# Tree attention on one core: where the last four heads' and one early quad's K and Q are transposed

## The chip, the cores and the metric

The kernel runs on one core of one Trainium2 chip. The metric is the device time of one execution in microseconds (us); of several executions the median is given. Engines are named as the profile names them: PE (TensorE, matmuls and transposes), PEld (its weight loads), DVE (VectorE), ACT (ScalarE), POOL (GpSimd, which here issues nearly all transfers), SP (SyncE).

## The reference, cut to what matters

Attention with 8 batches of 12 heads, 512 positions, 64 dimensions, in float32. A position attends to itself and to its ancestors in a binary heap.

```python
mask = np.zeros((seq, seq))
for i in range(seq):
    mask[i, i] = 1
    parent = i
    while parent > 0:
        parent = (parent - 1) // 2
        mask[i, parent] = 1
scores = np.einsum('bhqd,bhkd->bhqk', Q, K) * scale      # scale = 1/sqrt(64)
scores = scores + (1 - mask) * (-1e9)
weights = np.exp(scores - np.max(scores, axis=-1, keepdims=True))
weights = weights / (np.sum(weights, axis=-1, keepdims=True) + 1e-10)
return np.einsum('bhqk,bhkd->bhqd', weights, V)
```

## The kernel before

The 96 heads are worked on in **pairs** (two heads, index `i`, 0 to 47), **quads** (four heads, index `q`, 0 to 23, two pairs each) and **octets** (eight heads, index `o`, 0 to 11). Q, K and V are loaded from float32 into bf16 tiles of one octet each; K and Q come in halves of an octet, that is, by the quad. A position has at most nine keys that count, so a pair needs two score tiles only: one against the 128 keys nearest the root (`scores1`), one against a packed selection of the others (`scores2`). In each, a first matmul adds a mask code and a second adds the product of K and Q; ACT then takes the exponential of 128x1024 scores at once (lines 396 and 422).

For the scores, K and Q must lie with the dimension across the partitions. Both are brought there by transposes on PE, which write one PSUM tile, `kqp`, of two halves:

- `first_pair(i)` (the first 8 pairs, octets 0 and 1): 8 transposes of K and 8 of Q of one pair; DVE copies both halves to SBUF (line 322).
- `keys_of(q)` (from quad 4 on): 16 transposes of K for both pairs of a quad, line 308, one pair in each half of `kqp`; DVE copies the tile to `kT` (line 322).
- `queries_of(q)`: 16 transposes of Q for both pairs, line 357, into the second half of `kqp`; DVE copies that to `qT` (line 366).

There is one `kqp` tile, so each of these has to wait until DVE has copied out what the one before it wrote. In the last steps the space of `kqp` is also used for the output of pairs 45 and 47 (line 432).

`values(i)` multiplies the exponentials of pair i with V, which has to be spread out first to the packed order of the keys: POOL copies the top part (line 246), DVE the leaves (line 260) and a part of level 7 (lines 275 and 283), ACT the rest of level 7 (line 275). A column of ones beside V gives the sums, and `norm(i)` divides by them on DVE (lines 467 and 470). The output tile of `values` in PSUM is single too. `store` sends a quad's result out: POOL for most quads, SP and ACT for the last one.

The order of instructions on each engine is that in which the Python code issues them: the schedule is set by hand, and semaphores are put in where data demands them. One step `i` of the main loop issues the scores of pair i, a share of spreading on ACT, the values and the normalization of pair i-1, the transposes for pairs further ahead, a share of spreading on DVE, and then the next part of POOL's list of transfers. With the two conditions in lines 595 to 600, `keys_of(q)` comes in step 2q-3 and `queries_of(q)` in step 2q-2, both after the values and the normalization; quad q's first scores come in step 2q. So quad 4's K is issued in step 5 and quad 23's K and Q in steps 43 and 44.

Of the kernel before, what the change touches and what calls it, by code (L numbers as in the profile page):

```python
# [124 lines left out]
def kernel(  # L125
# [12 lines left out]
    NQ = B * H // 4  # L138
    NP = 2 * NQ
# [61 lines left out]
    OLD = 2  # L201
# [56 lines left out]
    def spread_leaves(o, upper, h0=0, h1=8):  # L258

        nc.vector.tensor_copy(  # L260
            out=tile_pair(o, 64 if upper else 0, h0, h1, upper),
            in_=vsts[o][64:128, h0:h1, upper:3 + upper:2, :],
        )
# [7 lines left out]
    def spread_l7(copy, o, quad, h0=0, h1=8):  # L271

        slot = 2 * (quad % 2)
        lower = quad < 2
        copy(  # L275
            out=tile_pair(o, 0, h0, h1, 1)[32 * quad:32 * quad + 32] if lower
            else tile_pair(o, 64, h0, h1, 0)[32 * quad - 64:32 * quad - 32],
            in_=swapped(vsts[o][32:64, h0:h1, slot + (not lower), :], D if lower else -D),
        )

    def spread_l7_over(o):

        nc.vector.tensor_copy(
            out=tile_pair(o, 64, 0, 8, 0),
            in_=swapped(vts[o % NV][0:64, 0:8, VCOL[3]:VCOL[3] + D], -D),
        )
# [23 lines left out]
    def transpose_keys(dst, i):  # L310
        for t in range(4):
            for a in range(2):
                transpose_one(dst, i, a, t, _slot_layout(t)[1], ksts, perms[t])

    def evac_units(name):
        kq = work.tile([P, 2, 16, 32], bf16, name=name)
        src = kqp[:, :, :]
        src = bass.AP(
            src.tensor, src.offset + 32 * _psum_unit(0),
            [list(src.ap[0]), [1024, 2], [32 * (_psum_unit(8) - _psum_unit(0)), 2], [1, 256]],  # L320
        )
        nc.vector.tensor_copy(  # L322
            out=kq[:, :, :, :].rearrange("p k (x y) c -> p k x (y c)", x=2), in_=src
        )
        return kq

    def first_pair(i):

        transpose_keys(kqp[:, 0, :], i)
        for t in range(4):  # L330
            for a in range(2):
                transpose_one(
                    kqp[:, 1, :], i, a, t, [_psum_unit(4 * QPOS[t] + j) for j in range(4)],
                    qsts, turns[:, :],
                )
        kq = evac_units("kq")
        kTs[i] = kq[:, 0, :, :]
        qTs[i] = kq[:, 1, :, :].rearrange("p (t u) c -> p t (u c)", t=4)

    def keys_of(q):  # L340

        for r in range(2):
            transpose_keys(kqp[:, r, :], 2 * q + r)
        kT = evac_units("kT")
        for r in range(2):
            kTs[2 * q + r] = kT[:, r, :, :]

    def queries_of(q):

        st = qsts[q // 2][:, 4 * (q % 2):4 * (q % 2) + 4, :, :].rearrange(  # L350
            "p (y x) t d -> p y (x t) d", y=2
        )
        for t in range(4):
            for j in range(2):
                for a in range(2):
                    dst = kqp[64 * a:64 * a + 64, 1, :]
                    nc.tensor.transpose(  # L357
                        out=bass.AP(
                            dst.tensor, dst.offset + 128 * QPOS[t] + 16 * j,
                            [list(dst.ap[0]), [512, 2], [32, 4], [1, 16]],  # L360
                        ),
                        in_=st[:, a, 4 * j + t, :],
                        identity=qperm,
                    )
        qT = work.tile([P, 2, 4, 128], bf16, name="qT")
        nc.vector.tensor_copy(  # L366
            out=qT[:, :, :, :].rearrange("p r t c -> p (r t c)"), in_=kqp[:, 1, :]
        )
        for r in range(2):
            qTs[2 * q + r] = qT[:, r, :, :]  # L370
# [10 lines left out]
    def scores1(i):  # L381

        sp = psS.tile([P, 2, 512], fp32, name="s1")
        for a in range(2):
            nc.tensor.matmul(  # L385
                out=sp[:, a, :], lhsT=k1code[64 * a:64 * a + 64, :],
                rhs=q1code[64 * a:64 * a + 64, :], start=True, stop=False,
            )
        for a in range(2):
            nc.tensor.matmul(  # L390
                out=sp[:, a, :], lhsT=keys(i, a, TOP),
                rhs=qTs[i][64 * a:64 * a + 64, :, :].rearrange("p t c -> p (t c)"),
                start=False, stop=True,
            )
        et = etpool.tile([P, 2, 4, 128], bf16, name="e1")
        nc.scalar.activation(  # L396
            out=et[:, :, :, :].rearrange("p a t c -> p (a t c)"),
            in_=natural(sp[:, :, :]),
            func=AF.Exp, scale=scale,
        )  # L400
        ets[i] = et

    def scores2(i):

        sp = psS.tile([P, 2, 4, 128], fp32, name="s2")
        for a in range(2):
            nc.tensor.matmul(  # L407
                out=sp[:, a, :, :].rearrange("p t c -> p (t c)"),
                lhsT=k2code[64 * a:64 * a + 64, :], rhs=q2code[64 * a:64 * a + 64, :],
                start=True, stop=False,  # L410
            )
        for tile2, lo, hi in ((2, 32, 192), (0, 192, 320), (1, 320, 384), (3, 416, 512)):
            for a in range(2):
                nc.tensor.matmul(  # L414
                    out=sp[:, a, :, :].rearrange("p t c -> p (t c)")[:, lo:hi],
                    lhsT=keys(i, a, TILE2[tile2]),
                    rhs=qTs[i][64 * a:64 * a + 64, :, :].rearrange("p t c -> p (t c)")[:, lo:hi],
                    start=False, stop=tile2 == 3, skip_group_check=tile2 in (2, 0),
                )
        e2 = etpool.tile([P, 2, 4, 128], bf16, name="e2")[:, :, :, :]  # L420
        e2s[i] = e2
        nc.scalar.activation(  # L422
            out=e2.rearrange("p a t c -> p (a t c)"),
            in_=natural(sp[:, :, :, :]),
            func=AF.Exp, scale=scale,
        )
# [50 lines left out]
    def store(eng, q, h0=0, n=4, step=1):  # L477
        eng.dma_start(  # L478
            out=Or[:, 4 * q + h0:4 * q + h0 + n:step, :],
            in_=ofs[q][:, h0:h0 + n:step, :, :].rearrange("p h t d -> p h (t d)"),  # L480
        )
# [39 lines left out]
    def spread_first(copy, quad, parts):  # L521

        for part in parts:
            if part < 4:
                spread_l7(copy, 0, part, 4 * quad, 4 * quad + 4)
            else:
                spread_leaves(0, part - 4, 4 * quad, 4 * quad + 4)
# [20 lines left out]
    def spread_scalar(i):  # L548

        if i == 1:  # L550
            spread_first(nc.scalar.copy, 1, (0, 1))
        o, quad = divmod(i + 1, 4)
        if 2 <= o < NO and quad == 0:
            spread_l7(nc.scalar.copy, o, 0)
        if i == 4:
            for quad in (0, 1):
                spread_l7(nc.scalar.copy, 1, quad)

    def pool_until(done, wanted):
        while done < wanted:  # L560
            next(program, None)
            done += 1
        return done
# [14 lines left out]
    for i in range(NP + 1):  # L578
        if i < NP:
            scores1(i)  # L580
            scores2(i)
            spread_scalar(i)
        if i == 1:
            first_pair(2)
            spread_first(nc.vector.tensor_copy, 1, (2, 3))
        if i >= 1:
            values(i - 1)
            norm(i - 1)
        if i >= 8 and i % 4 == 0 and i < NP:
            spread_l7_over(i // 4)  # L590

        for n in (1 if i == 0 else i + 2,):
            if n < 4 * OLD:
                first_pair(n)
        q, r = divmod(i + 3, 2)
        if 2 * OLD <= q < NQ and r == 0:
            keys_of(q)
        q, r = divmod(i + 2, 2)
        if 2 * OLD <= q < NQ and r == 0:
            queries_of(q)  # L600
        if i == 0:
            spread_first(nc.vector.tensor_copy, 0, range(6))
        spread_vector(i)
        if steps < NO:
            steps = pool_until(steps, min((i + 11) // 4, NO))
        else:
            steps = pool_until(steps, min(steps + 2, NO + (i - 2) // 2 - (NQ - 1 - BEHIND)))
        if i == NP - 1:
            store(nc.sync, NQ - 1, 0, 3, 2)
# [32 lines left out]
```

## Time and profile before

| what | value |
|---|---|
| median of 5 runs (lowest, highest) | 136.88 us (135.82, 138.01) |
| the profiled execution's own time | 136.5 us |
| its span in the trace | 134.7 us |
| PE busy, of the span | 115.6 us (86%) |
| DVE busy | 103.8 us (77%) |
| ACT busy | 105.7 us (78%) |
| POOL busy | 95.2 us (71%) |
| one exponential (line 396), mean | 1018 ns |
| one evacuation of K (line 322, kT), mean | 684 ns |
| one evacuation of Q (line 366), mean | 686 ns |
| bytes moved by the DMA engines | 32.20 MB |

How to read it: a busy share is over the whole span, and PE's end times are modelled, so it isn't PE at its peak. "L308 MATMUL kqp<-ptile,kst x16" is a group of 16 instructions of line 308 that write `kqp` and read `ptile` and `kst`; what stands in brackets is the time its engine sat idle before it and what ended that. The slices of the page are 40 equal parts of the span, each 3.37 us; a digit 9 means busy for 90% or more. The chain of work that ended last is followed back from the last instruction.

### The profile page before, as it was taken

The page shows a single profiled execution, that of the slowest core. Times are in us where ns is not written, and L with a number is a line of the kernel's source. Part 1 is how long each engine was busy: PE and PEld are TensorE (multiplying, and loading weights), DVE is VectorE, ACT ScalarE, POOL GpSimd, SP SyncE. Part 2 cuts the span into 40 slices and gives each one's busy share as a digit, 9 for nine tenths or more (in the row PEclk, how much of TensorE's full clock was granted, in tenths as well). Part 3 has the DMA queues.
Part 4 walks back from the last instruction along what each step waited for, and adds up shares of the span by engine and source line. Part 5 has one row for each costly group of instructions (what it writes and reads, how often), then busy time and mean ns, then how long its engine had stood idle before and what let it go on. Part 6 is the DMA issues. An engine that isn't in the chain of part 4 may idle for free.

```text
span 134.7 us, 5515 instructions
## 1 busy us (share of the span) xinstructions
PE 115.6 (86%) x2409; PEld 79.8 (59%) x2409; DVE 103.8 (77%) x218; ACT 105.7 (78%) x113; POOL 95.2 (71%) x140
## 2 busy tenths in 40 slices
PE   4986996599999998998998999999996988969920
PEld 1434674467576776766675675767664765746610
DVE  5548989568969879798789789798797689659450
ACT  4155989479799799899799797997985997879920
POOL 6939989598697974984886697596696498295100
PEclk9999999999999999999999999999999999999998
DMA  3999999999999999999999999999999999999982
GB/s 105 230 165 192 191 196 201 199 204 195 202 198 227 334 203 212 338 210 204 338 218 201 318 242 199 298 263 200 286 274 202 263 297 201 249 382 364 373 297 90
DMA packets 36858, 32.20 MB, mean 239 GB/s; under 512 B 1458, under 2 KB 33890, under 8 KB 36834
## 3 DMA queue, kind: packets, MB, share of 16 engines
q0 software_dynamic: 35520, 30.68, 120.5%
q1 hardware_dynamic: 754, 0.72, 1.7%
q10 hardware_dynamic: 560, 0.46, 1.1%
q8 instruction: 19, 0.31, 0.8%
q14 instruction: 5, 0.04, 0.1%
HBM read 37.88 MB, written 12.58 MB: 375 GB/s over the span
## 4 chain that ended last, share of the span: by engine, by line
DMA 43%; PE 24%; DVE 11%; ACT 7%; POOL 6%; issue 5%; ACTq 0%; POOLq 0%
DMA vst<-in_V_dram 26%; DMA kst<-in_K_dram 9%; DMA qst<-in_Q_dram 8%; PE ob L441 8%; PE kqp L308 4%; ACT e L396 4%; DVE of L470 4%; ACT e L422 4%; PE s L385 3%; PE s L407 3%; PE s L390 2%; PE s L414 2%; POOL kst L220 2%; DVE vt L275 2%; PE kqp L357 2%
## 5 line engine op out<-in xcount | busy, mean ns | idle before, releaser
L396 ACT ACTIVATE e<-s 128x1024 bf16<-128x1024 f32 x48 | 48.8, 1018 | 17.8 <-PE s L390 17.6
L422 ACT ACTIVATE e<-s 128x1024 bf16<-128x1024 f32 x48 | 48.6, 1013 | 0.0
L441 PE MATMUL ob<-vt,e 128*128 128x65 bf16 (+1 forms) x920 | 37.1, 197 | 1.2 <-DVE vt L275 0.9
L246 POOL COPY vt<-vst 32x512 bf16<-32x512 bf16 (+1 forms) x52 | 30.9, 595 | 10.0 <-DMA vst<-in_V_dram 8.1
L441 PEld LDWEIGHTS <-e 128*128 128x128 bf16 (+1 forms) x960 | 30.5, 102 | 7.9 <-issue 1.0
L470 DVE TENSOR_TENSOR of<-ob,rec 128x512 f32<-128x512 f32 x46 | 31.8, 692 | 1.6
L220 POOL DMA_DIRECT2D kst<-in_K_dram x24 | 18.8, 784 | 11.4 <-DMA vst<-in_V_dram 9.1
L478 POOL DMA_DIRECT2D out_dram<-of x23 | 17.5, 767 | 4.8 <-DVE of L470 4.2
L308 PE MATMUL kqp<-ptile,kst 128*64 128x128 bf16 x384 | 16.2, 222 | 5.3 <-DMA kst<-in_K_dram 2.3
L407 PE MATMUL s<-codes 64*128 64x512 bf16 x96 | 18.5, 378 | 2.1 <-ACT e L422 1.9
L467 DVE RECIPROCAL rec<-ob 128x8 f32<-128x8 f32 x46 | 9.6, 208 | 13.9 <-PE ob L441 13.1
L385 PE MATMUL s<-codes 64*128 64x512 bf16 x96 | 18.9, 390 | 0.5
L308 PEld LDWEIGHTS <-kst 128*64 128x64 bf16 x384 | 12.7, 111 | 7.7 <-DMA kst<-in_K_dram 4.5
L414 PEld LDWEIGHTS <-kT 64*128 64x128 bf16 x320 | 13.3, 94 | 6.0
L322 DVE COPY kT<-kqp 128x1024 bf16<-128x1024 bf16 x20 | 13.7, 684 | 2.9 <-PE kqp L308 2.8
L236 POOL DMA_DIRECT2D qst<-in_Q_dram x20 | 14.1, 707 | 2.4 <-issue 1.1
L407 PEld LDWEIGHTS <-codes 64*128 64x128 bf16 x96 | 7.4, 94 | 14.0 <-issue 8.4
L390 PE MATMUL s<-qT,kT 64*128 64x512 bf16 x80 | 15.3, 376 | 0.0
L414 PE MATMUL s<-qT,kT 64*128 64x160 bf16 (+3 forms) x320 | 14.7, 209 | 0.0
L275 ACT COPY vt<-vst 32x1024 bf16<-32x1024 bf16 (+1 forms) x14 | 13.6, 970 | 1.3 <-DMA vst<-in_V_dram 1.3
L220 POOL DMA_DIRECT2D vst<-in_V_dram x13 | 11.7, 904 | 4.1 <-DMA qst<-in_Q_dram 1.3
L366 DVE COPY qT<-kqp 128x1024 bf16<-128x1024 bf16 x20 | 13.7, 686 | 0.3
(34 smaller groups left out, 96.7 us busy)
## 6 DMA issues: line engine op xcount, KB each, us to landing
out_dram<-of POOLq DMA_DIRECT2D x23, 512.0 KB, 10.6
kst<-in_K_dram POOLq DMA_DIRECT2D x23, 256.0 KB, 11.3
qst<-in_Q_dram POOLq DMA_DIRECT2D x23, 256.0 KB, 9.7
vst<-in_V_dram POOLq DMA_DIRECT2D x11, 512.0 KB, 12.5
vst<-in_V_dram POOLq DMA_DIRECT2D x2, 256.0 KB, 7.5
first_k<-in_K_dram SPq DMA_DIRECT2D x1, 256.0 KB, 3.2
first_q<-in_Q_dram ACTq DMA_DIRECT2D x1, 256.0 KB, 4.1
out_dram<-of SPq DMA_DIRECT2D x1, 256.0 KB, 3.7
```

Of the source, the lines that this page charges most:

```text
L220: nc.gpsimd.dma_start(out=kept[o][:, h0:h0 + n:step, :, :].rearrange("p h t d -> p h (t d)"), in_=src[:, 8 * o + h0:8 * o + h0 + n:step, :],)
L246: eng.tensor_copy(out=vts[o % NV][32 * j:32 * j + 32, h0:h1, VTOP:VTOP + D], in_=vsts[o][0:32, h0:h1, UNITS[TOP + j][1], :],)
L308: nc.tensor.transpose(out=dst, in_=st[i // 4][:, head(i, a), t, :], identity=perm)
L385: nc.tensor.matmul(out=sp[:, a, :], lhsT=k1code[64 * a:64 * a + 64, :], rhs=q1code[64 * a:64 * a + 64, :], start=True, stop=False,)
L390: nc.tensor.matmul(out=sp[:, a, :], lhsT=keys(i, a, TOP), rhs=qTs[i][64 * a:64 * a + 64, :, :].rearrange("p t c -> p (t c)"), start=False, ...
L396: nc.scalar.activation(out=et[:, :, :, :].rearrange("p a t c -> p (a t c)"), in_=natural(sp[:, :, :]), func=AF.Exp, scale=scale,)
L407: nc.tensor.matmul(out=sp[:, a, :, :].rearrange("p t c -> p (t c)"), lhsT=k2code[64 * a:64 * a + 64, :], rhs=q2code[64 * a:64 * a + 64, :] ...
L414: nc.tensor.matmul(out=sp[:, a, :, :].rearrange("p t c -> p (t c)")[:, lo:hi], lhsT=keys(i, a, TILE2[tile2]), rhs=qTs[i][64 * a:64 * a + 6 ...
L422: nc.scalar.activation(out=e2.rearrange("p a t c -> p (a t c)"), in_=natural(sp[:, :, :, :]), func=AF.Exp, scale=scale,)
L441: nc.tensor.matmul(out=ob[lo:hi, a, start_o:start_o + 65], lhsT=e[:, a, QPOS[t], lo:hi], rhs=vt[:, head(i, a), col:col + 65], **flags,)
L470: nc.vector.tensor_tensor(out=ofs[q][:, r:r + 3:2, :, :], in0=vals, in1=rec[:, :, :, :].to_broadcast([P, 2, 4, D]), op=ALU.mult,)
L478: eng.dma_start(out=Or[:, 4 * q + h0:4 * q + h0 + n:step, :], in_=ofs[q][:, h0:h0 + n:step, :, :].rearrange("p h t d -> p h (t d)"),)
```

## The change

Two steps of transposing that the two general conditions placed are now placed by themselves.

- Quad 4 (pairs 8 and 9, `4 * OLD - 2` is 6): `keys_of(4)` leaves step 5 and is issued in step 6, between the scores of pair 6 and the values of pair 5. `queries_of(4)` stays in step 6 behind the normalization of pair 5.
- Quad 23 (pairs 46 and 47): `keys_of(23)` leaves step 43 and is issued in step 44 (`NP - 4`), behind the values and the normalization of pair 43. `queries_of(23)` leaves step 44 and is issued in step 45 (`NP - 3`), between the scores of pair 45 and the values of pair 44.

Where a transposing step goes, its evacuation on DVE goes with it. No instruction is added or removed, and nothing of ACT's, POOL's and SP's order is touched.

```diff
@@ -583,21 +583,28 @@
         if i == 1:
             first_pair(2)
             spread_first(nc.vector.tensor_copy, 1, (2, 3))
+        if i == 4 * OLD - 2:
+            keys_of(2 * OLD)
+        elif i == NP - 3:
+            queries_of(NQ - 1)
         if i >= 1:
             values(i - 1)
             norm(i - 1)
         if i >= 8 and i % 4 == 0 and i < NP:
             spread_l7_over(i // 4)
 
+
         for n in (1 if i == 0 else i + 2,):
             if n < 4 * OLD:
                 first_pair(n)
         q, r = divmod(i + 3, 2)
-        if 2 * OLD <= q < NQ and r == 0:
+        if 2 * OLD < q < NQ - 1 and r == 0:
             keys_of(q)
         q, r = divmod(i + 2, 2)
-        if 2 * OLD <= q < NQ and r == 0:
+        if 2 * OLD <= q < NQ - 1 and r == 0:
             queries_of(q)
+        if i == NP - 4:
+            keys_of(NQ - 1)
         if i == 0:
             spread_first(nc.vector.tensor_copy, 0, range(6))
         spread_vector(i)
```

## The prediction

> **What bounds the kernel now.** I read the slices of the page first: is a transfer limit in force all the time?
>
> ```profile
> DMA  3999999999999999999999999999999999999982
> GB/s 105 230 165 192 191 196 201 199 204 195 202 198 227 334 203 212 338 210 204 338 218 201 318 242 199 298 263 200 286 274 202 263 297 201 249 382 364 373 297 90
> HBM read 37.88 MB, written 12.58 MB: 375 GB/s over the span
> ```
>
> The DMA engines are busy from the second slice to the last but one. Pure loads show about 200 GB/s because they arrive as bf16, half the bytes read. So the moment at which the last load lands is set by the bytes ahead of it, not by the engines. The chain in order of time agrees, and tells where this ends:
>
> ```profile
> 93.96 13.08 DMA vst<-in_V_dram
> ...
> 107.33 12.07 DMA kst<-in_K_dram
> 119.40 0.04 issue
> 119.44 0.64 PE kqp L308 x16
> ```
>
> The last K load (heads 4 to 7 of octet 11, that is, pairs 46 and 47) lands at 119.40 us; then computation is on the chain to the end. Next the timeline of PE around it (start, us, instruction, idle before it):
>
> ```profile
> 117.35 0.79 PE L441 MATMUL ob<-vt,e 128*128 128x65 bf16 x20
> 119.44 0.64 PE L308 MATMUL kqp<-ptile,kst 128*64 128x128 bf16 x16 [1.30 <-DMA kst<-in_K_dram]
> 120.01 0.39 PE L385 MATMUL s<-codes 64*128 64x512 bf16 x2
> ```
>
> PE stands 1.30 us before the K transposes for pairs 46 and 47, and pair 44's scores, which need nothing of that load, stand behind them. ACT shows what that is worth:
>
> ```profile
> 117.88 1.02 ACT L422 ACTIVATE e<-s 128x1024 bf16<-128x1024 f32 x1
> 118.78 1.03 ACT L275 COPY vt<-vst 32x1024 bf16<-32x1024 bf16 x1
> 120.72 1.02 ACT L396 ACTIVATE e<-s 128x1024 bf16<-128x1024 f32 x1 [0.91 <-PE s L390]
> 124.76 1.02 ACT L396 ACTIVATE e<-s 128x1024 bf16<-128x1024 f32 x1
> ```
>
> Only 0.91 of the 1.30 us is idle time of ACT; the copy of line 275 fills the rest. The line at 124.76 is pair 46, the first that needs the late load. Last, DVE in the same stretch, since both evacuations of the late heads go through it:
>
> ```profile
> 120.12 0.69 DVE L322 COPY kT<-kqp 128x1024 bf16<-128x1024 bf16 x1 [1.01 <-PE kqp L308]
> 120.84 0.42 DVE L260 COPY vt<-vst 64x1024 bf16<-64x1024 bf16 x1
> 121.28 0.72 DVE L275 COPY vt<-vst 32x1024 bf16<-32x1024 bf16 x1
> 122.03 0.21 DVE L467 RECIPROCAL rec<-ob 128x8 f32<-128x8 f32 x1
> 122.27 0.69 DVE L470 TENSOR_TENSOR of<-ob,rec 128x512 f32<-128x512 f32 x1
> 122.99 0.42 DVE L283 COPY vt<-vt 64x1024 bf16<-64x1024 bf16 x1
> 123.44 0.69 DVE L366 COPY qT<-kqp 128x1024 bf16<-128x1024 bf16 x1
> ```
>
> After the K load DVE has no gap until the Q evacuation ends at 124.13. It will be the next limit.
>
> **What the Trainium skill says.** (1) "TensorE: Matmul & The Clock Gate", Step-by-step: what each phase is for: matmuls stay in program order, only weight loads are pulled ahead. The trace agrees: nothing overtakes the transposes waiting at 119.44. (2) "SBUF — State Buffer", SBUF: two separate sides: VectorE in a two-port mode and GpSimd take one port pair in turn, the later one standing still. Line 283's ten copies take 421 to 766 ns, line 260's 26 (two widths) 291 to 743, which fits but doesn't prove it; this is my range for those copies. (3) "DMA: Bandwidth & Descriptors", Anatomy of one DMA: some 2 us of a transfer are fixed, mostly waiting until the last byte is confirmed. The last store, 128 KB, took 3.0 us from issue: the end follows the last normalization by about that.
>
> **The change, part by part.** The profiled execution took 136.5 us, 1.8 more than its span of 134.7; the median is 136.88, so the profile ran 0.4 faster than the median.
>
> *K step of quad 4 (pairs 8 and 9), from the end of step 5 to between scores and values of step 6.* Before, its 16 transposes waited 1.18 us (start 26.28) for the evacuation of pair 7, and pair 6's scores stood behind; exp of pair 6 began at 27.56. Now the scores go first: pair 7's transposes start at 24.49 and need 0.57, then 0.61 for scores and 0.10 to ACT: exp at about 25.8. The new wait, the same one until 26.28, has pair 5's values behind it: 26.85 to 27.57. DVE does the K evacuation 26.96 to 27.65 ahead of the normalization; the Q transposes, which reuse the same PSUM tile, wait for that: 27.69 to 28.24, then pair 7's scores, exp at 28.24+0.61+0.10 = 28.95 instead of 29.68. So 0.73 us of lead from pair 7 on. I value it at nothing at the end: PE later stands for K at 108.42 (0.66 us), 113.56 (0.38) and 119.44, times that saturated transfers set. No DMA is issued by the moved step, and POOL's order of issues stays. If that cover were gone, up to 0.73 us would reach the end; a loss I exclude, as pairs 6 and 7 both come earlier.
>
> *K step of quad 23, from step 43 to behind step 44's values.* Removed: the 1.30 us wait. PE: values of pair 42 end issue at 118.07; scores1 of pair 44 follow; scores2 wait for the exp that ends at 118.90, start 118.94, and values of pair 43 start 0.52 later (as 122.71 to 123.23): 119.46 to 120.18. The transposes then start at 120.18, 0.8 after the load has landed: no wait. ACT: exp(44) starts when the copy ends, 119.83, not 120.72: 0.89 earlier. Then at its pace of 0.92 per exp: 120.75, exp1(45) 121.67, exp2(45) 122.59 to 123.61.
>
> DVE's order changes too. The normalization of pair 42 ends at 119.11; the two spread copies (0.42+0.72) no longer wait for the K evacuation: 119.14 to 120.30. Normalization of pair 43 starts 120.33, line 283 follows 0.96 later (122.03 to 122.99 before): 121.29, then the K evacuation at 121.74 to 122.43. It is now the one that is late.
>
> *Q step of quad 23, from behind step 44's values to between step 45's scores and values.* Its transposes write the half of the tile that the K evacuation reads, so they wait until 122.47; behind them on PE stand values of pair 44 and everything after. They run 0.62, to 123.09; evacuation 123.13 to 123.82. Values of pair 44 start 0.55 after the transposes, 123.02, issue until 123.74; scores1 of pair 46: codes 123.74, keys from 123.97 (qT is there), end 124.35; exp at 124.45. Before it was 124.76. Of the 0.89 us **only 0.31 is left**: ACT idles from 123.5 to 124.45.
>
> From there: exp2(46) 125.37, exp1(47) at 126.29 (back to back; scores1 of 47 are ready at 126.12), exp2(47) 127.21 to 128.23. Before it ended at 128.72: 0.49 earlier, because the small gap ahead of pair 47 closes too. The last 16 value matmuls, the normalization and the ACT store follow as before: last store at 129.96 instead of 130.45.
>
> *Stores.* Q 21's store goes out right behind the three at 120.26 to 122.50 instead of 123.25, Q 22's at about 126.7 instead of 127.41. The windows of 1 us show DMA share 0.70 from 128 to 129: there is a hole to fill. From 120 to 133 the moved bytes sum to 4.29 MB; at the 373 GB/s of the eight slices from 120 to 128 that is 11.5 us, to 131.5, where traffic now ends near 132.2. So 0.7 us is the most that the drain allows, and 0.49 fits.
>
> *Bounds.* The unknown is how long the three spread copies take at their new places, beside POOL's copies (117.57 to 120.30) and store issues. I take 0.42, 0.72, 0.42. With line 275 at 0.43 as well, the gain is about 0.8; with all three at 0.74, 0.74 and 0.77 it is 0.49−0.69 = −0.2.
>
> Sum: −0.49 on 136.5 is 136.0 in the profile; on the median, **136.4**.
>
> **Rivals.**
> 1. *The early lead reaches the end.* For it: PE is 95% busy from 30 to 97 us, so in a run in which transfers are quicker, computation is the limit and 0.73 counts in full. Against: the three waits for K at the end. 136.9−0.49−0.73 = **135.7**.
> 2. *The store drain decides.* Traffic is already at 360 to 380 GB/s from 120 to 128; earlier stores fill just the hole, 30% of 1 us. 136.9−0.3 = **136.6**.
> 3. *Slower: DVE's spread copies.* They now stand ahead of the K evacuation, between 119.1 and 121.7, of which POOL's copies overlap the first 1.2 us. If they take 0.49 us more together than I took, pair 46 gets nothing earlier at the end; at their longest rows, 0.69 more, the end is 0.2 later: **137.1**. For it: line 275 took 0.74 at 110.32, with POOL copying, and line 260 0.62 at 98.66. Against: line 260 took 0.42 at 117.48 beside the same copies.
>
> That nothing is changed is excluded: the waited-for instruction is really moved.
>
> **How the numbers follow.** Forecast 0.50, rival 1 0.20, rival 2 0.15, rival 3 0.15. Single runs of the kernel spread from 135.82 to 138.01, so a median of a few runs is good to about 0.5. Range: from 0.3 below rival 1 to 0.2 above rival 3, 135.4 to 137.3. About 1% (1.4 us: below 135.5 or above 138.2) is what a measurement can tell from no change. Below lies a half of rival 1 and the lucky edge of the forecast, 0.17; above, an outer part of rival 3, 0.07; the rest 0.76.
>
> **What would show it.** In the trace after: no wait for K on PE near 119 us; exp(44) at the copy's end; a new gap on ACT of 0.5 to 1 us ahead of pair 46; DVE without a gap between 119 and 122.4; the early gap of 2.30 us on ACT near 27.5 mostly gone, with a wait for K near 113 that is longer by the lead. I'm wrong if the last K lands at another time than about 119.4 (then the early step reaches the transfers), if DVE's copies stretch, or if the last store lands over 3.5 us after its issue.

## The result and the profile after

The changed kernel takes 136.46 us (median of 44 runs, 135.86 to 138.09), the kernel before 136.57 (79 runs beside them). The ratio is 0.9999, with a 95% interval of 0.9986 to 1.0012: **no change**. The ratio leaves out the few executions in a slower state and isn't the quotient of the two medians. The forecast of 136.4 and its range hold the time, but the 0.36% that it saw as likeliest lies outside the interval, so a step of the sum was wrong. The profiled execution took 135.86 us, its span is 134.1.

This execution began its work earlier than that of before: pair 5's first exponential, ahead of every changed instruction, starts at 22.55 instead of 23.32 us. So I count the tail from **the mark**, the start of quad 22's K transposes, which wait for a load in both: 113.56 before, 112.62 after.

The slices of the page, as shown for before:

```profile
DMA  2999999999999999999999999999999999999992
GB/s 88 247 184 196 195 196 201 200 201 197 202 198 242 319 203 216 341 206 201 344 214 199 330 231 199 310 256 196 287 275 200 264 298 200 249 381 373 365 327 72
HBM read 37.88 MB, written 12.58 MB: 376 GB/s over the span
```

The transfers are as full as before. The chain in order of time (start, us, what):

```profile
101.66 10.91 DMA kst<-in_K_dram
112.57 0.04 issue
112.62 0.64 PE kqp L308 x16
...
121.20 0.70 DVE kT L322
121.95 0.64 PE kqp L357 x16
```

The K load at its end is now that of quad 22; quad 23's K load has left the chain, and DVE's evacuation of K has come into it. PE's timeline:

```profile
119.15 0.62 PE L308 MATMUL kqp<-ptile,kst 128*64 128x128 bf16 x16
...
121.95 0.64 PE L357 MATMUL kqp<-ptile,qst 128*64 128x128 bf16 x16 [0.62 <-DVE kT L322]
```

Quad 23's K transposes wait for nothing (before: 1.30 us for the load), but its Q transposes wait 0.62 us for DVE. ACT in the same stretch:

```profile
117.84 1.03 ACT L275 COPY vt<-vst 32x1024 bf16<-32x1024 bf16 x1
118.78 1.01 ACT L396 ACTIVATE e<-s 128x1024 bf16<-128x1024 f32 x1
...
123.95 1.02 ACT L396 ACTIVATE e<-s 128x1024 bf16<-128x1024 f32 x1 [1.45 <-PE s L390]
```

And DVE:

```profile
118.20 0.80 DVE L260 COPY vt<-vst 64x1024 bf16<-64x1024 bf16 x1
119.02 0.74 DVE L275 COPY vt<-vst 32x1024 bf16<-32x1024 bf16 x1
119.79 0.21 DVE L467 RECIPROCAL rec<-ob 128x8 f32<-128x8 f32 x1
120.03 0.69 DVE L470 TENSOR_TENSOR of<-ob,rec 128x512 f32<-128x512 f32 x1
120.75 0.42 DVE L283 COPY vt<-vt 64x1024 bf16<-64x1024 bf16 x1
121.20 0.69 DVE L322 COPY kT<-kqp 128x1024 bf16<-128x1024 bf16 x1
```

The 0.91 us that ACT lost ahead of pair 44 are gone, and 1.45 us ahead of pair 46 have come. DVE has no gap, as forecast, but line 260's copy takes 0.80 instead of the 0.42 I took. From the mark, pair 46's first exponential starts 11.33 us later (before 11.20), and the last store is issued 16.83 us later (before 16.89). So the computation's end moved by 0.06 us where 0.49 were forecast.

And even where the computation does end earlier, the span doesn't follow. The store of quad 22 is the last big one (512 KB). This is its time from issue to landing, in the view of the output's transfers. Before, where it is issued at 127.41:

```profile
DMA to landing us min/median/max: 4.6/4.6/4.6
```

After, where it is issued at 126.25:

```profile
DMA to landing us min/median/max: 5.3/5.3/5.3
```

From the mark it is issued 13.85 us later before and 13.63 after, but it lands 18.49 and 18.95 us after it (127.41 and 4.64, 126.25 and 5.32, less the mark). So an earlier issue did not make it land earlier.

### The profile page after: what moved, and what is told of

Read it like the earlier page. It is cut to its first block, busy times and chain, and to the rows that moved or that the text cites. A ratio compares the mean times of both kernels' runs of the same rounds, so it can differ in the third digit from the quotient of the medians.

```text
span 134.1 us, 5514 instructions
## 1 busy us (share of the span) xinstructions
PE 116.1 (87%) x2409; PEld 80.3 (60%) x2409; DVE 103.8 (77%) x218; ACT 105.8 (79%) x113; POOL 95.0 (71%) x140
## 4 chain that ended last, share of the span: by engine, by line
PE 39%; DMA 26%; DVE 13%; ACT 9%; issue 5%; POOL 4%; ACTq 0%; POOLq 0%
PE ob L441 11%; DMA vst<-in_V_dram 10%; DMA qst<-in_Q_dram 8%; DMA kst<-in_K_dram 8%; PE kqp L308 6%; ACT e L422 5%; PE s L407 5%; PE s L385 4%; ACT e L396 4%; PE s L390 3%; PE s L414 3%; DVE of L470 3%; PE ob L292 3%; PE kqp L357 3%; DVE kq L322 3%
```

## The experiments

Two theories came out of this. **DVE theory**: VectorE's spread copies, slowed beside GpSimd's, used up the gain, and the computation sets the end. **Drain theory**: the stores that are still queued set the end, whatever the computation does. Each run is compared with the kernel before, timed beside it (median 136.74 us for the first eight, 136.59 for the last two).

### Each half alone

`early_only` leaves out the changes for quad 23, `late_only` those for quad 4:

```diff
# early_only, from the changed kernel
-        elif i == NP - 3:
-            queries_of(NQ - 1)
-        if 2 * OLD < q < NQ - 1 and r == 0:
+        if 2 * OLD < q < NQ and r == 0:
             keys_of(q)
-        if 2 * OLD <= q < NQ - 1 and r == 0:
+        if 2 * OLD <= q < NQ and r == 0:
             queries_of(q)
-        if i == NP - 4:
-            keys_of(NQ - 1)
# late_only, from the changed kernel
-        if i == 4 * OLD - 2:
-            keys_of(2 * OLD)
-        elif i == NP - 3:
+        if i == NP - 3:
             queries_of(NQ - 1)
-        if 2 * OLD < q < NQ - 1 and r == 0:
+        if 2 * OLD <= q < NQ - 1 and r == 0:
             keys_of(q)
```

> Only quad 4's K step is moved; quad 23 stays as before. Transfer theory: pair 6's first exponential comes about 1.8 us and pair 7's 0.7 us earlier, PE then waits longer for K near the end, the last K lands at the same time, and the time is that of before within 0.2 us (136.4 to 136.8). Lead theory (the lead reaches the end): about 0.7 us faster, 135.9.

> Only quad 23's K and Q steps are moved. DVE theory (VectorE's two spread copies, slowed beside GpSimd's, hold up the late K evacuation): a gap of about 1.4 us on ACT ahead of pair 46 and no gain, 136.4 to 136.7, as with the whole change. My prediction's sum would give 136.1. Drain theory (the last stores set the end): 136.5 as well, so this run tells only whether the two halves cancel each other.

Measured: early half 136.85 us, ratio 0.9994 (0.9971 to 1.0017); late half 136.73, ratio 0.9983 (0.9954 to 1.0011). Neither does anything clear of noise, so it isn't two halves that cancel, as far as intervals of up to 0.5% can tell. The lead theory's 0.7 us (0.995) is outside the first interval. PE's waits for loads in the early half alone, from the list of waits (in all, times, longest):

```profile
PE kqp L308 <- DMA kst<-in_K_dram: 4.7, 7, 1.8
```

Before, they were 2.3 us in 3 waits: the lead is turned into waiting for K. Its size varies: counted from pair 5's exponential, pair 6's comes 1.53 us and pair 7's 0.41 us earlier here, where about 1.8 and 0.7 were expected. In `late_only` the late copies look as after: 0.80 and 0.74 us, and a gap of 1.44 us on ACT ahead of pair 46.

### The computation's end made earlier, in three ways

`k_evac_first` puts quad 23's K step, with its evacuation, ahead of the normalization of pair 43; PE's order stays. `no_leaf_copy` leaves out the slow copy of line 260. `no_pool_copy` leaves out GpSimd's four copies that ran beside it.

```diff
# k_evac_first
             values(i - 1)
+            if i == NP - 4:
+                keys_of(NQ - 1)
             norm(i - 1)
...
-        if i == NP - 4:
-            keys_of(NQ - 1)
# no_leaf_copy, in spread_vector
             for part in parts:
+                if i == NP - 5 and part == 1:
+                    continue
# no_pool_copy, in pool_program
-            if q == NQ - BEHIND + 1:
-                spread_top(nc.gpsimd, NO - 1)
```

> The whole change, but quad 23's K evacuation goes ahead of pair 43's normalization on VectorE. DVE theory: the evacuation begins some 1.3 us earlier, the Q transposes find the tile free, ACT's gap ahead of pair 46 shrinks from 1.45 to about 0.8 us, and the time falls by 0.4 to 0.6 us, to 136.0. Drain theory: the gap shrinks in the same way and the time stays at 136.5.

> The whole change with one spread copy of line 260 left out in step 43 (the second leaf copy of octet 11, so some values of the last octet are taken from an older one). DVE theory: pair 43's normalization and quad 23's K evacuation come 0.4 us earlier, and so does the end: 136.1. Drain theory: they come earlier and the time stays at 136.5.

> The changed kernel without GpSimd's four copies of line 246 for octet 11 (the top part of the last octet's V is taken from an older one). Port theory: line 260's copy in step 43 takes 0.42 us instead of 0.80, line 275's 0.42 instead of 0.74. GpSimd then has no wait for V, and the stores of quads 18 and 19 go out up to 2.8 us earlier. Drain theory: neither moves the end, 136.3 to 136.6, as the slowest DMA engine has work all the time. Compute theory: 0.5 us faster, 136.0.

Measured, in this order: 136.44 us, ratio 0.9988 (0.9965 to 1.0012); 136.49, 0.9982 (0.9959 to 1.0004); 136.71, 1.0001 (0.9976 to 1.0025). All three do what they should on the engines. With the evacuation first, ACT's gap is 0.76 us:

```profile
124.62 1.02 ACT L396 ACTIVATE e<-s 128x1024 bf16<-128x1024 f32 x1 [0.76 <-PE s L390]
```

Without GpSimd's copies, the two DVE copies take the short time:

```profile
118.95 0.42 DVE L260 COPY vt<-vst 64x1024 bf16<-64x1024 bf16 x1
119.39 0.42 DVE L275 COPY vt<-vst 32x1024 bf16<-32x1024 bf16 x1
```

So what slowed them is GpSimd's work beside them. It is the copies and not the store issues behind them: in `after_3_less`, below, no store is issued there and the two take 0.81 and 0.74. But the time doesn't follow. From the mark to ACT's last store issue, and to the end of the span, each in one profiled execution:

| kernel | mark, us | to the last store's issue | to the end of the span |
|---|---|---|---|
| before | 113.56 | 16.89 | 21.2 |
| changed | 112.62 | 16.83 | 21.5 |
| late_only | 113.21 | 16.82 | 21.5 |
| no_leaf_copy | 113.34 | 16.40 | 21.9 |
| no_pool_copy | 113.37 | 16.40 | 21.7 |
| k_evac_first | 113.97 | 16.15 | 21.8 |

The last store is issued up to 0.74 us earlier than before, and the span doesn't end earlier for it. Nor does the time fall: if the computation set the end, 0.74 us would be a ratio of 0.9946 and 0.49 us one of 0.9964; the intervals of `k_evac_first` and `no_pool_copy` exclude theirs, that of `no_leaf_copy` just doesn't. The two runs with 0.42 us copies, or one copy fewer, reach just the 16.40 that my sum had (129.96 less 113.56). What the end waits for is seen in the DMA view of `k_evac_first` from 126 to 136 us (40 slices of 0.25 us, mean share of the 16 DMA engines):

```profile
DMA  9999999898799999898999951111000000000000
```

From 132 us on, 10 to 20% of the engines, two or three of 16, still work for one more microsecond. For each of these transfers the trace has sixteen completion times. I take them as one for each of the 16 engines. For the last K load before, the first is at 114.79 and the last at 119.40: the last engine is 4.6 us behind the first. The last completion of each of the nine stores that POOL issues behind the loads (quads 14 to 22), in us:

```
before        121.70 123.00 124.29 125.59 126.89 128.17 129.47 130.77 132.05
changed       120.99 122.29 123.60 124.90 126.19 127.47 128.77 130.06 131.57
k_evac_first  122.87 124.16 125.44 126.74 128.04 129.33 130.62 131.92 133.21
```

The engine that is last finishes one store every 1.3 us (one step of 1.51 apart) from the last loads to the end, without a hole. When the stores are issued makes no difference to it. Nor does it get faster when others fall idle: before, from 128 to 129 us, the mean share was 0.70, so that nearly a third of the engines had nothing to do, and its step from 128.17 to 129.47 is 1.30 us like the others. That speaks for its own rate as the limit, against that of all engines together.

### Fewer bytes to drain

If that is the limit, taking stores away must make the end earlier, and then the order on DVE must count. Three kernels without the stores of quads 18 to 20:

```diff
             yield
-            store(nc.gpsimd, q)
+            if q not in (18, 19, 20):
+                store(nc.gpsimd, q)
```

> The kernel before without the stores of quads 18, 19 and 20 (1.5 MB of the output are not written). Drain theory (the slowest of the 16 DMA engines always has stores to work off, 1.3 us for each 512 KB, up to the end): 3.9 us of its work are gone, the computation becomes the limit, and the end comes about 1 us after what the last store needs by itself: 135.3 to 135.8. Compute theory (the last normalization sets the end already, with a fixed time for the store behind it): 136.5, no change.

> The changed kernel without the stores of quads 18, 19 and 20. Drain theory: as the kernel before without them, since the last store is issued only 0.06 us earlier from the K landing on: 135.3 to 135.8. If my prediction's 0.49 us were there, it would be 0.5 below that kernel.

> The changed kernel with quad 23's K evacuation ahead of pair 43's normalization, without the stores of quads 18, 19 and 20. Drain theory: with the drain shortened, the 0.7 us that this order brings at the last store show at last: 0.5 to 0.8 us below the changed kernel without them, about 134.8. Compute theory: nothing, since the same order brought nothing with all stores.

| without three stores | median, us | ratio to before, 95% interval | mark to the last store's issue | to the end of the span |
|---|---|---|---|---|
| kernel before | 135.87 | 0.9937 (0.9906 to 0.9968) | 16.77 | 20.6 |
| changed kernel | 136.07 | 0.9935 (0.9911 to 0.9958) | 16.84 | 20.4 |
| K evacuation first | 135.15 | 0.9882 (0.9843 to 0.9921) | 16.13 | 19.7 |

The first two gain 0.9 us by the ratio, though 3.9 us of the slowest engine's work are gone: now the computation is the limit. From issue to landing the last store takes 2.85, 2.57 and 2.54 us in these three traces, where it took 3.00 before and 4.30 in `k_evac_first`. The drain has a hole, in the DMA view of the last of these kernels from 118 to 136 us (slices of 0.45 us):

```profile
DMA  9999999987773399931000599979294000000000
```

And the evacuation order, worth nothing clear of noise with all stores, is now worth 0.0053 of 136.74, 0.7 us; the trace has 0.71 (16.84 less 16.13). The two intervals just overlap; taken together the difference is 0.0053 with some 0.0046 either way, so it is only just clear of noise. Changed and unchanged kernel stay alike here too, as their last stores do. So two things stood in the way of the 0.49 us, one behind the other.

### One engine, or the sum of the bytes

Last, whether the slowest engine counts or the whole: the same 393 KB of added loads, spread on 8 rows or on 16.

```diff
+    spare = consts.tile([P, 6144], fp32, name="spare")
+    Krows = K.rearrange("b h s d -> (b h) (s d)")
...
+        if i in (20, 28):
+            nc.scalar.dma_start(out=spare[0:8, :], in_=Krows[0:8, 0:6144])
```

> The changed kernel with two added loads of 8 partitions by 24 KB, 393 KB together, issued by ACT in steps 20 and 28 into a spare tile that nothing reads. Slowest-engine theory (each of the 16 DMA engines works off its own share and the most loaded one sets the end): 8 rows go to 8 engines at most, 49 KB each, at 375/16 = 23.4 GB/s 2.1 us for each; the end is 2.1 us later, 138.6, if the slowest is one of them, and less than 1 us if it is not. Total theory (only the sum of the bytes counts): 393 KB at 375 GB/s, 1.05 us later, 137.5. Compute theory: the transfers have room and the time stays at 136.5.

> The same 393 KB as two loads of 16 partitions by 12 KB. Slowest-engine theory: 24.6 KB for each of 16 engines, 1.05 us later, 137.5, half of what the 8 rows cost. Total theory: 137.5 as well, the same as with 8 rows. Compute theory: 136.5.

Measured: 141.95 us, ratio 1.0391 (1.0356 to 1.0426), with 8 rows; 139.59, 1.0234 (1.0205 to 1.0263), with 16. (The other kernel has 16 rows by 3072 elements.) The same bytes cost 5.4 us (141.95 less 136.59) on 8 rows and 3.0 on 16, 1.8 times as much: the total theory, equal costs, falls, and so does the compute theory. The sizes are not mine: 2.6 and 2.9 times the expected 2.1 and 1.05. The records of single packets give a part of it: the sixteen of 24 KB took 2.23 us each and the thirty-two of 12 KB 0.63, so two of them, if they fall on one engine, are 4.5 and 1.25 us. The rest, 0.9 and 1.7 us, stays unexplained. The cost comes in with the loads, not only with the stores: quad 22's K lands at 118.71 us with 8 rows and at 115.25 with 16, where it was 113.52 before, each in one execution. The prediction had it that the bytes ahead of a load set when it lands; here the same bytes give two different times. These loads also put long packets where short ones ran, so the pair of runs shows that the share per engine counts, but not that it alone does.

## Why the prediction was right or wrong

The prediction read from the chain that "computation is on the chain to the end". This is the last piece of that chain, before:

```profile
129.72 0.69 DVE of L470
```

It is over at 130.41 us, 4.3 us before the span is. The landing of the stores is not on the chain, so the chain can't tell what the end waits for. The steps one by one:

- **K step of quad 4**: right, in size too. Counted from pair 5's exponential, pair 6's comes 1.86 us earlier (1.78 forecast) and pair 7's 0.75 (0.73). The lead is 0.43 at pair 28 and gone at pair 36; from 86.70 us on PE waits for K. So it is used up earlier than forecast: the wait for K near 113 is not longer by the lead (0.39 us, before 0.38). "I value it at nothing at the end" holds, by `early_only` too.
- **K step of quad 23, PE and ACT**: right. PE doesn't wait for the load, and pair 44's exponential starts at the end of the copy. The new gap ahead of pair 46 was forecast as 0.5 to 1 us and is 1.45, for the next reason.
- **DVE's order**: right in kind, with a gain that mostly vanishes. Wrong in one term: "I take 0.42, 0.72, 0.42" for the spread copies; they took 0.80, 0.74 and 0.42. That is the 0.40 us by which the K evacuation starts later than in my sum (8.58 us from the mark, not 8.18), and with it 0.43 of the 0.49 us is gone. Rival 3 had the mechanism, its place and its price; the copies took 0.40 us more, just short of the 0.49 from which pair 46 gains nothing at the end. I had what I needed for it: line 260's 743 ns maximum, and what I had cited of the Trainium skill, "SBUF — State Buffer", SBUF: two separate sides, that of VectorE in a two-port mode and GpSimd, which share a port pair, the later one stands still. The 0.80 and 0.74 us beside GpSimd's copies, against 0.42 without them, fit that, though no run here shows the ports themselves. I let one favourable row, 0.42 at 117.48, decide. There the copy began 0.09 us before GpSimd's; the late one began in the midst of them.
- **Stores**: this step failed. "0.7 us is the most that the drain allows, and 0.49 fits" was worked out from the mean rate of 16 engines and a hole in their mean share. The hole was on the engines that were ahead; the slowest had none. The room for an earlier end was not 0.7 us but nothing that shows: 0.74 us of earlier computation in `k_evac_first` gave 0.9988 (0.9965 to 1.0012). Rival 2 was the right one, and its 0.3 us was too much as well, from the same mean share.
- **"That nothing is changed is excluded"**: wrong, and it is what came out. That the instruction waited for is really moved shows that the engines' times change, not that the end does. Of the three signs of being wrong, one is clear: DVE's copies stretched. The last store landed 3.23 us after its issue, under the 3.5 named, and so didn't give the drain away; the last K load landed 5.95 us after the mark, before 5.84.
- The **median** of the five runs shown, 136.88, was 0.3 above that of 79 runs. This has put the forecast near the measured time by luck: the gain was 0.0, not 0.5.

No version tried here with all its stores is faster than the kernel before by more than the noise: as long as the slowest DMA engine has work up to the last store, an earlier end of the computation didn't show in the time.

## What to carry to other kernels

When transfers are saturated to the end, ask what the slowest of the DMA engines has left, not what their mean share leaves: a store that takes the longer to land the earlier it is issued (quad 22's: 4.6, 5.3 and 6.3 us, issued 13.85, 13.63 and 12.95 us after the mark in three kernels) says that what is queued ahead of it decides. Before working on the computation's tail, leave out some of the last stores once; if the time then falls, the tail isn't yet the limit. And price a VectorE copy that is moved by what GpSimd does at its new place, not by the row of its old one.

## What was not expected of the hardware

- The 16 DMA engines drift apart by some us although each of the big transfers has its sixteen completions, and first and last move on at the same 1.3 us for most of the time: in the kernel before, first and last completion of one load lie 2.1 us apart at 12 us, 2.7 at 59, 4.0 at 110 and 4.6 at 119. The gap grows in a few steps of 0.3 to 0.8 us. The instruction loads (0.31 MB in 19 packets, each 0.9 to 1.0 us long) come one at a time and would do that, but this is argued only; no run tried it.
- A packet of 24 KB took 2.23 us on average, one of 12 KB 0.63: half the size in less than a third of the time.
- Line 260's and line 275's copies on VectorE take 0.80 and 0.74 us beside GpSimd's copies and 0.42 each without them, in the same place of the kernel. Store issues on GpSimd may do it too: before, line 275's copy took 0.72 at 121.28, when GpSimd's copies were over (120.30) and it was issuing stores (120.26 to 122.50). Without these stores, in `before_3_less`, it took 0.42, the line below. Line 260's copy beside the same issues, at 120.84, took 0.42, so not every copy is slowed; no run was made to settle this.

```profile
120.76 0.42 DVE L275 COPY vt<-vst 32x1024 bf16<-32x1024 bf16 x1
```
